# Attention softmax pacing, the start of the last value products and the cut of the last output half tile in a one-core hybrid layer step

## The chip, the cores and the metric

The kernel runs on one core of a Trainium2 chip. The core has TensorE (PE in the profile; its weight loads are PEld), VectorE (DVE), ScalarE (ACT), GpSimd (POOL) and SyncE (SP), each with its own queue of instructions, which it works through in order. SBUF is the on-chip memory of 128 partitions; PSUM holds what PE writes, in eight banks of 128 x 512 floats. The metric is the device time of one execution in microseconds; 613.63 us is the median of three runs before the change (612.94 to 613.96).

## The reference

One layer of a diffusion trunk: 1024 latent tokens and 128 own context tokens of width 1024, and 256 cached context tokens. A shared normalised and modulated input goes through one projection into a gated MLP group (A) and a latent attention group with four heads (B); both are gated, concatenated, sent through one output projection, added to the residual under a gate, and normalised. The change concerns the attention of the latent tokens and the very end of the output projection:

```python
def one_block(i):
    qn = lax.dynamic_slice_in_dim(q_nope, s0, Q_BLOCK, axis=1)
    logits = []
    for qr, (kn, kr, _) in zip(q_ropes, key_sets):      # latent keys, cached context keys
        logits.append(jnp.einsum('bqhn,bkhn->bhqk', qn, kn) + jnp.einsum('bqhr,bkr->bhqk', qrb, kr))
    s = jnp.concatenate(logits, axis=-1).astype(jnp.float32) * ATTN_SCALE
    p = jax.nn.softmax(s, axis=-1).astype(v_all.dtype)
    return jnp.einsum('bhqk,bkhv->bqhv', p, v_all)
...
y = jnp.concatenate([a_out, attn * jax.nn.silu(g_b)], axis=-1) @ w_o
return x + gate * y
...
y_prompt = _rmsnorm(xp, final_g)
```

## The kernel before

**Precision.** Every large product is made of three: each operand is split into a high part in the shorter format fp32r (`pool_copy` on POOL or a copy on ACT) and a low part, the rest (`lo_of` on DVE, line 112), and high x high, high x low and low x high are added up in PSUM.

**Written time.** The order of instructions on PE, ACT, DVE and POOL is written out by the program. A counter `now` stands for the time that PE has used so far: each step of PE adds its cost. `later(dt, fn)` puts work of the other engines on a list, due at the step's start plus dt; `catch_up` writes out what is due before the next step. So a number such as 0.6 or 2.3 does not delay anything on the chip: it decides only between which other instructions of its engine something stands. `need(key)` writes out the list, in order of due time, until the named result has been written. `merged(a, b)` interleaves two lists of steps by their shares of the cost. SP's queue of DMAs is in written order as well.

**Attention.** There are 8 tiles of 128 queries and 4 heads, 32 heads `(t, h)` in all, and 16 pairs of two heads `(t, pr)`. A round `c` of the main loop (line 1964 on) scores heads 2c+2 and 2c+3 and does the value products of pair c-1. Scoring a head is `lat(0)`, `lat(1)` (512 latent keys each, five products) and `con` (256 context keys, lines 1520 to 1524). Then `start` takes the maximum over the latent logits and `shift` that over the context logits and the bias `nb` (DVE); `exp(0)` and `exp(1)` (ACT, line 1498) write the context and the latent part of `e`, a tile of 128 x 1280, with their sums; `divide` adds the sums, takes the reciprocal (DVE) and scales `e` (POOL, line 1506). Value products of a pair go in five steps `tr(i)` and `av(i)`: `tr` transposes four blocks of `e` on PE into a PSUM bank (`pT`, line 1567; the pool `pst` has two banks, shared with the `at` products), ACT copies the high part `ph` out (line 1571), DVE makes the low part `pl`, which empties the bank; `av` (lines 1591 to 1593) lags two steps behind `tr`. `fin1` copies the sum to `os`, `fin2` multiplies it by the value projection (`at`, line 1610), and DVE multiplies the result into `mixB` (line 1612).

**Units.** From round 2 on, 16 small units (`t_unit`) prepare differences of blocks of the output weights for the last stage (a Strassen scheme); each `divide` takes one off the list `units` until it is empty. While the list is not empty, or for tile 1, the exponentials are written "apart". Later the lists `his` and `los` hold high and low parts of other splits (pieces of `w_o`, first blocks of the mixed activations); `spare_hi(n)` and `spare_lo(n)` write out up to n of them, `divide` among their callers. `need_lo` and `wo_need` write out what a product is about to read.

**The change of stage.** After the last scored head the loop ends, `need` asks for the `e` of the last two heads, the score banks are closed and five banks `psw` opened for the output projection. `tail` is then set, which lets every `low()` of a transposed block call `spare_hi` and `spare_lo`. The first output products (`early`) are interleaved with the value products of pairs 14 and 15 (tile 7). Pieces 5 to 7 of `w_o` are loaded into buffers that the attention gives free, and split in halves of 512 columns.

**The end.** The last stage is planned by a small list scheduler, `Plan`: each step has an engine, a cost, what it depends on and a priority, and the plan's run sets the order on each engine. The last products are those of the prompt tile's left half (`finish_left`): tile 8, columns 0 to 511, in two parts cut at `cut_at` (steps `pz0`, `pz1`, 24 products each). Each part is multiplied by the gate (`zm`, line 2298), added to x (`za`, line 2299), squared and summed on ACT (`sq8.0` and `zq`, lines 2103 and 2304), and multiplied by the final gain (`zf`, line 2307); `zv` (line 2308) to `zr3` make the root, `zo0` and `zo1` scale both halves and store them.

Of the kernel before, what the change touches and what calls it, by code (L numbers as in the profile page):

```python
# [20 lines left out]
NS = 8  # L21
# [73 lines left out]
def tile_hymba_step(ctx: ExitStack, tc: tile.TileContext, I, O):  # L95
# [1375 lines left out]
    def softmax(t, h, lat_, con_):  # L1471
# [11 lines left out]
        def shift():  # L1483
            V.tensor_reduce(m[:, 1:2], con_, axis=AX.X, op=ALU.max)
            if units or t < 2 or (t, h) == (NS - 1, 3):
                V.tensor_reduce(nb, m, axis=AX.X, op=ALU.max)
                V.tensor_scalar(nb, nb, nscl[:, t : t + 1], None, op0=ALU.mult)  # L1487
            else:
                V.scalar_tensor_tensor(nb, m[:, 0:1], m[:, 1:2], nscl[:, t : t + 1], op0=ALU.max, op1=ALU.mult)
            apart = bool(units) or t == 1  # L1490
            later(1.2 if apart else 0.6, lambda: exp(0))
            later(2.3 if apart else 0.6, lambda: exp(1))
            later(3.9 if apart else 3.1 if t == 0 else 2.5, divide)
            later(1.3, lambda: spare_lo(1))
# [5 lines left out]
        def divide():  # L1500
            V.tensor_tensor(rs, su[:, 0:1], su[:, 1:2], op=ALU.add)
            V.reciprocal(rs, rs)
            first = 512 if (t, h) == (NS - 1, 3) else 0
            if first:
                V.tensor_scalar(e[:, :first], e[:, :first], rs, None, op0=ALU.mult)
            G.tensor_scalar(e[:, first:], e[:, first:], rs, 0.0, op0=ALU.mult, op1=ALU.add)  # L1506
            made.add(("e", t, h))
# [18 lines left out]
    def score_steps(t, h):  # L1526
# [16 lines left out]
        def con():  # L1543
            logits(c_, (a, b, unrot), slice(CTX0, CTX0 + 256))
            later(0.95 if units or t == 1 else 0.7, cell["shift"])

# [4 lines left out]
    def value_steps(t, pr):  # L1551
# [9 lines left out]
        def tr(i):  # L1561
# [11 lines left out]
            def low():  # L1573
                lo_of(pl[:, :w], ps[:, :w], ph[:, :w])
                made.add(("p", t, pr, i))
                if tail:
                    spare_hi(1)
                    spare_lo(1)
# [75 lines left out]
    def next_load():  # L1654
# [16 lines left out]
        def ready():  # L1671
            for i in range(2):
                c_ = slice(i * 512, i * 512 + 512)
                split_job(lambda c_=c_: pool_copy(hi[:, c_], r[:, c_]), lambda c_=c_: low(c_), ("w", k, i))
# [118 lines left out]
    with tc.manual_schedule(engines=engines):  # L1793
# [170 lines left out]
        for c in range(len(pairs)):  # L1964
# [20 lines left out]
            if 2 * c + LEAD + 1 == 23:  # L1985
                for k in range(3):
                    wo_piece(2 + k, *flat[1][2 * k : 2 * k + 2])
        need(*[("e", *h) for h in heads[-2:]])
        closed(c_ps)
# [24 lines left out]
        later(2.0, lambda: [t_pieces(2, 2 * n, whole[2][:, 2048 * n + 2048 : 2048 * n + 4096]) for n in range(2)])  # L2014
        vs = value_stream(pairs[-2])
        merged(vs[:3], [])
        merged(vs[3:], early[:10])
# [258 lines left out]
    def finish_left():  # L2276
# [6 lines left out]

        cut_at = 384
        own_of = (slice(0, cut_at), slice(cut_at, 512))
# [8 lines left out]
        for j in range(2):  # L2294
            o = lambda j=j: cell[j][:, at_[j]]
            dur = (0.57, 0.3)[j]
            on_t(f"pz{j}", (4.3, 1.6)[j], lambda j=j: left(j), [], takes=("w",) if j else ("w", "w"))
            on_v(f"zm{j}", lambda o=o, c=own_of[j]: V.tensor_tensor(o(), o(), g()[:, c], op=ALU.mult), [f"pz{j}", "own0"], 0.5, dur)
# [7 lines left out]
        for j, dep in ((0, ["za1"]), (1, ["zv"])):  # L2306
            on_v(f"zf{j}", lambda j=j: V.tensor_tensor(x()[:, own_of[j]], cell[j][:, at_[j]], fg[:, own_of[j]], op=ALU.mult), [*dep, "sq8.0", "zq", "fg"] if j else [*dep, "sq8.0", "fg"], 0.6, (0.57, 0.3)[j])
        on_v("zv", lambda: V.scalar_tensor_tensor(v, ssq[(8,)][:, 2:3], 1.0 / 1024.0, v0, op0=ALU.mult, op1=ALU.add), ["zq", "zv1"], 0.4, 0.2)
# [125 lines left out]
```

## Time and profile before

| what | value |
|---|---|
| median of 3 runs | 613.63 us |
| lowest, highest | 612.94, 613.96 us |
| the profiled execution, as a run | 614.5 us |
| its span in the trace | 612.7 us |
| its mean granted PE clock | 0.992 of full speed |
| ACT, DVE, POOL busy | 330.2, 426.1, 208.4 us |
| attention stage, from the first `pT` of a pair to the last value product | about 334 to 528 us |
| last products `left`, first and last start | 598.63, 605.34 us |

The profile is of one execution, and its times count from the start of its span. A row of the timeline gives the start, the duration, the engine, the line of the kernel, the operation, output and inputs with their shapes, how many instructions are merged, and in brackets the time that the engine stood idle before it, with what ended the wait. Products on PE overlap, so the distance between two starts, not the duration, is what one costs. A row of the view by stretches gives the stretch, its length, the busy time and the number of instructions of PE, PEld, DVE, ACT and POOL, then the granted clock, the DMA share and GB/s.

### The profile page before, as it was taken

What the parts mean: (1) busy time and instruction counts of PE and PEld (TensorE: products, weight loads), DVE (VectorE), ACT (ScalarE), POOL (GpSimd) and SP (SyncE); (2) the same over time, 40 slices, a digit from 0 to 9 for tenths busy, and PEclk for the clock granted to TensorE, in tenths of its full rate; (3) what the DMA queues carried; (4) which work ended last, traced back from release to release, by engine and by line L of the source; (5) the groups of instructions that cost most, each with busy time, mean ns of one, the idle gap of its engine ahead of it and who ended that gap; (6) DMA issues with size and microseconds to landing.
All of it is one profiled execution on the core that took longest, in us unless ns stands there. A gap on an engine that the chain in (4) does not pass through costs nothing.

```text
span 612.7 us, 10225 instructions
## 1 busy us (share of the span) xinstructions
PE 599.2 (98%) x3671; PEld 542.2 (88%) x3671; DVE 426.1 (70%) x937; ACT 330.2 (54%) x765; POOL 208.4 (34%) x249
## 2 busy tenths in 40 slices
PE   7999999999999999999999999999999999999995
PEld 6777889999988999999998999999989988888885
DVE  4685467997756468466778677777678875577885
ACT  5555773335433244465577656665745553357543
POOL 2452103000000000243363354545434446359833
PEclk9899999999999999999999999999999999999999
DMA  8992010100351114100002033434231118951443
GB/s 311 390 393 81 0 35 2 35 0 1 138 207 70 70 62 167 41 1 1 1 8 70 1 112 114 150 125 139 70 120 70 35 70 293 330 201 42 147 152 141
DMA packets 31059, 67.33 MB, mean 110 GB/s; under 512 B 3344, under 2 KB 17440, under 8 KB 29984
## 3 DMA queue, kind: packets, MB, share of 16 engines
q1 hardware_dynamic: 27792, 55.93, 25.8%
q0 software_dynamic: 2352, 8.39, 4.1%
q10 hardware_dynamic: 864, 2.36, 1.2%
q8 instruction: 29, 0.48, 0.3%
q14 instruction: 22, 0.18, 0.1%
HBM read 53.45 MB, written 13.21 MB: 109 GB/s over the span
## 4 chain that ended last, share of the span: by engine, by line
PE 92%; DMA 2%; DVE 2%; ACT 1%; issue 1%; SPq 0%; ACTq 0%; DVEq 0%
PE p L954 9%; PE tp L752 8%; PE pT L1567 6%; PE tp L976 6%; PE s L1520 3%; PE o L1591 3%; PE s L1523 3%; PE s L1521 3%; PE s L1522 3%; PE s L1524 3%; PE o L1593 3%; PE o L1592 3%; PE zacc L1390 2%; PE zacc L1389 2%; PE zacc L1391 2%; PE S L1928 2%
## 5 line engine op out<-in xcount | busy, mean ns | idle before, releaser
L112 DVE TENSOR_TENSOR pl<-pT,ph 128x512 fp32r<-128x512 f32 x81 | 55.5, 687 | 38.0 <-ACT ph L1571 37.8
L1506 POOL TENSOR_SCALAR e<-e,rs 128x1280 f32<-128x1280 f32 (+1 forms) x32 | 46.9, 1466 | 101.4 <-ACT ph L1571 41.5
L1498 ACT ACTIVATE e<-s,nb,scl 128x256 f32<-128x256 f32 x64 | 56.5, 885 | 34.5 <-DVE nb L1487 18.9
L1571 ACT CAST ph<-pT 128x512 fp32r<-128x512 f32 x80 | 46.4, 589 | 42.7 <-PE pT L1567 42.0
L1237 POOL TENSOR_TENSOR kr<-z,rope 128x64 f32<-128x64 f32 x8 | 2.6, 324 | 172.1 <-ACT z L1246 172.1
L752 PE MATMUL tp<-area,w 128*128 128x384 f32 x288 | 52.4, 338 | 0.0
L752 PEld LDWEIGHTS tp<-area,w 128*128 128x128 f32 x288 | 50.3, 188 | 0.4
L1567 PE MATMUL pT<-ident,e 128*128 128x128 f32 x320 | 48.2, 273 | 1.9 <-DVE pl L112 1.9
L1591 PE MATMUL o<-ph,vh 128*128 128x256 f32 x160 | 48.2, 301 | 0.0
L1593 PE MATMUL o<-ph,vl 128*128 128x256 f32 x160 | 45.1, 282 | 0.0
L1592 PE MATMUL o<-pl,vh 128*128 128x256 f32 x160 | 45.0, 281 | 0.0
L1567 PEld LDWEIGHTS pT<-ident,e 128*128 128x128 f32 x320 | 37.5, 141 | 5.2 <-DVE pl L112 1.3
L1481 DVE TENSOR_REDUCE m<-s 128x1 f32<-128x1024 f32 x32 | 38.9, 1216 | 2.6 <-PE s L1524 2.6
L1520 PE MATMUL s<-kch,area 128*128 128x512 f32 (+2 forms) x100 | 39.2, 392 | 0.0
L1521 PE MATMUL s<-kcl,area 128*128 128x512 f32 (+2 forms) x100 | 35.3, 353 | 0.0
L1523 PE MATMUL s<-krh,area 128*128 128x512 f32 (+2 forms) x100 | 35.3, 353 | 0.0
L1522 PE MATMUL s<-kch,area 128*128 128x512 f32 (+2 forms) x100 | 35.2, 352 | 0.0
L1524 PE MATMUL s<-krl,area 128*128 128x512 f32 (+2 forms) x100 | 35.1, 351 | 0.0
L976 PE MATMUL tp<-area,w 128*128 128x384 f32 x192 | 35.0, 337 | 0.0
L976 PEld LDWEIGHTS tp<-area,w 128*128 128x128 f32 x192 | 33.6, 187 | 0.4 <-issue 0.4
L1591 PEld LDWEIGHTS o<-ph,vh 128*128 128x128 f32 x160 | 30.1, 188 | 1.6
L1592 PEld LDWEIGHTS o<-pl,vh 128*128 128x128 f32 x160 | 30.2, 189 | 1.4
(696 smaller groups left out, 1726.6 us busy)
## 6 DMA issues: line engine op xcount, KB each, us to landing
ada<-in_ada_ss SPq DMA_DIRECT2D x16, 512.0 KB, 8.0
w2r<-in_w_t SPq DMA_DIRECT2D x12, 512.0 KB, 4.3
x<-in_x SPq DMA_DIRECT2D x9, 512.0 KB, 7.4
adag<-in_ada_g SPq DMA_DIRECT2D x4, 1024.0 KB, 4.9
traw<-in_w_o SPq DMA_DIRECT2D x16, 256.0 KB, 3.1
tdram<-thi SPq DMA_DIRECT2D x32, 128.0 KB, 1.8
tdram<-traw SPq DMA_DIRECT2D x32, 128.0 KB, 1.8
wor<-in_w_o SPq DMA_DIRECT2D x8, 512.0 KB, 3.7
```

Of the source, the lines that this page charges most:

```text
L112: V.tensor_tensor(lo, src, f32(hi), op=ALU.subtract)
L752: T.matmul(tps[i, g][:, :GW], w_[i][:, k, :], x_[k, g], start=k == 0 and j == 0, stop=k == NK - 1 and j == 2)
L954: T.matmul(banks[key], a_, b_, start=k == 0 and m == 0, stop=k == 3 and m == len(passes) - 1)
L976: T.matmul(tps[c, 2][:, :GW], w_[c][:, k, :], x_[k, 2], start=k == 0 and m == 0, stop=k == NK - 1 and m == 2)
L1498: S.activation(e[:, sl], src, AF.Exp, bias=nb, scale=scl[:, t : t + 1], accum_out=su[:, i : i + 1])
L1520: T.matmul(ps, qh_, kch[:, sl], start=True, stop=False)
L1521: T.matmul(ps, qh_, kcl[:, sl], start=False, stop=False)
L1523: T.matmul(ps, qr_, krh[:, sl], start=False, stop=False)
L1567: T.transpose(ps[:, w : w + P], es[t, h][:, c * P : (c + 1) * P], ident)
L1591: T.matmul(o, vh[:, kt, :], ph[:, sl], start=c == 0, stop=False)
L1592: T.matmul(o, vh[:, kt, :], pl[:, sl], start=False, stop=False)
L1593: T.matmul(o, vl[:, kt, :], ph[:, sl], start=False, stop=c == n - 1)
```

## The change

There are three groups of edits, and the arithmetic that is done stays the same.

1. In `softmax` and `con` the spaced times now hold for every tile but the first, whether or not units are left: `shift` 0.95 (0.7 before) after the step of `con`, then `exp(0)` 1.2 (0.6), `exp(1)` 2.3 (0.6), `divide` 3.9 (2.5). For the very last head `exp(0)` is due after 0.5.
2. The first three steps of pair 14 (tile 7, first two heads) are written before `need` asks for the last division, and so before the `psw` banks are opened and `tail` is set. The last division is POOL's alone (DVE had done 512 of its 1280 columns). In the tail `low()` writes out two high parts instead of one, and pieces 5 to 7 of `w_o` are split right half first.
3. The left half of the last tile is cut at 256 instead of 384 columns, and the plan's costs for its steps are set to match.

```diff
--- before.py
+++ after.py
@@ -1487,8 +1487,9 @@
                 V.tensor_scalar(nb, nb, nscl[:, t : t + 1], None, op0=ALU.mult)
             else:
                 V.scalar_tensor_tensor(nb, m[:, 0:1], m[:, 1:2], nscl[:, t : t + 1], op0=ALU.max, op1=ALU.mult)
-            apart = bool(units) or t == 1
-            later(1.2 if apart else 0.6, lambda: exp(0))
+            apart = t > 0
+            last = (t, h) == (NS - 1, 3)
+            later(0.5 if last else 1.2 if apart else 0.6, lambda: exp(0))
             later(2.3 if apart else 0.6, lambda: exp(1))
             later(3.9 if apart else 3.1 if t == 0 else 2.5, divide)
             later(1.3, lambda: spare_lo(1))
@@ -1500,10 +1501,7 @@
         def divide():
             V.tensor_tensor(rs, su[:, 0:1], su[:, 1:2], op=ALU.add)
             V.reciprocal(rs, rs)
-            first = 512 if (t, h) == (NS - 1, 3) else 0
-            if first:
-                V.tensor_scalar(e[:, :first], e[:, :first], rs, None, op0=ALU.mult)
-            G.tensor_scalar(e[:, first:], e[:, first:], rs, 0.0, op0=ALU.mult, op1=ALU.add)
+            G.tensor_scalar(e, e, rs, 0.0, op0=ALU.mult, op1=ALU.add)
             made.add(("e", t, h))
             spare_hi(1 if his and his[0] in heavy else 2)
             spare_lo(2)
@@ -1542,7 +1540,7 @@
 
         def con():
             logits(c_, (a, b, unrot), slice(CTX0, CTX0 + 256))
-            later(0.95 if units or t == 1 else 0.7, cell["shift"])
+            later(0.95 if t else 0.7, cell["shift"])
 
         return [(1.08, lambda: lat(0)), (1.08, lambda: lat(1)), (0.55, con)]
 
@@ -1574,7 +1572,7 @@
                 lo_of(pl[:, :w], ps[:, :w], ph[:, :w])
                 made.add(("p", t, pr, i))
                 if tail:
-                    spare_hi(1)
+                    spare_hi(2)
                     spare_lo(1)
 
             later(1.15, low)
@@ -1669,7 +1667,7 @@
                 next_load()
 
         def ready():
-            for i in range(2):
+            for i in range(2) if k < 5 else (1, 0):
                 c_ = slice(i * 512, i * 512 + 512)
                 split_job(lambda c_=c_: pool_copy(hi[:, c_], r[:, c_]), lambda c_=c_: low(c_), ("w", k, i))
 
@@ -1985,6 +1983,8 @@
             if 2 * c + LEAD + 1 == 23:
                 for k in range(3):
                     wo_piece(2 + k, *flat[1][2 * k : 2 * k + 2])
+        vs = value_stream(pairs[-2])
+        merged(vs[:3], [])
         need(*[("e", *h) for h in heads[-2:]])
         closed(c_ps)
         c_pw, psw = opened("psw", bufs=5, space=PSUM)
@@ -2012,8 +2012,6 @@
         early += [(0.65, lambda k=k: product(2, first_banks[2], ks=[k])) for k in range(3)]
         later(0.5, lambda: early_split(2))
         later(2.0, lambda: [t_pieces(2, 2 * n, whole[2][:, 2048 * n + 2048 : 2048 * n + 4096]) for n in range(2)])
-        vs = value_stream(pairs[-2])
-        merged(vs[:3], [])
         merged(vs[3:], early[:10])
         merged(value_stream(pairs[-1], drain=True), early[10:])
         catch_up(1e9)
@@ -2281,7 +2279,7 @@
         g, x = (lambda: own[0][:, 0:512]), (lambda: own[0][:, 512:1024])
         on_g("z4", lambda: G.tensor_tensor(keep, keep, fg[:, R], op=ALU.mult), ["sq8.1", "fg"], 2.5)
 
-        cut_at = 384
+        cut_at = 256
         own_of = (slice(0, cut_at), slice(cut_at, 512))
         at_ = (slice(0, cut_at), slice(0, 512 - cut_at))
 
@@ -2293,8 +2291,8 @@
 
         for j in range(2):
             o = lambda j=j: cell[j][:, at_[j]]
-            dur = (0.57, 0.3)[j]
-            on_t(f"pz{j}", (4.3, 1.6)[j], lambda j=j: left(j), [], takes=("w",) if j else ("w", "w"))
+            dur = 0.43
+            on_t(f"pz{j}", 2.9, lambda j=j: left(j), [], takes=("w",) if j else ("w", "w"))
             on_v(f"zm{j}", lambda o=o, c=own_of[j]: V.tensor_tensor(o(), o(), g()[:, c], op=ALU.mult), [f"pz{j}", "own0"], 0.5, dur)
             on_v(f"za{j}", lambda o=o, c=own_of[j]: V.tensor_tensor(o(), o(), x()[:, c], op=ALU.add), [f"zm{j}"], 0.5, dur)
         square(8, 0, lambda: cell["junk"][:, own_of[0]], L, ["za0"], 0.5, lambda: cell[0][:, own_of[0]])
@@ -2304,7 +2302,7 @@
             "zq", lambda: S.activation(cell["junk"][:, own_of[1]], cell[1][:, at_[1]], AF.Square, accum_out=ssq[(8,)][:, 2:3]), ["za1"], 0.4, 0.5
         )
         for j, dep in ((0, ["za1"]), (1, ["zv"])):
-            on_v(f"zf{j}", lambda j=j: V.tensor_tensor(x()[:, own_of[j]], cell[j][:, at_[j]], fg[:, own_of[j]], op=ALU.mult), [*dep, "sq8.0", "zq", "fg"] if j else [*dep, "sq8.0", "fg"], 0.6, (0.57, 0.3)[j])
+            on_v(f"zf{j}", lambda j=j: V.tensor_tensor(x()[:, own_of[j]], cell[j][:, at_[j]], fg[:, own_of[j]], op=ALU.mult), [*dep, "sq8.0", "zq", "fg"] if j else [*dep, "sq8.0", "fg"], 0.6, 0.43)
         on_v("zv", lambda: V.scalar_tensor_tensor(v, ssq[(8,)][:, 2:3], 1.0 / 1024.0, v0, op0=ALU.mult, op1=ALU.add), ["zq", "zv1"], 0.4, 0.2)
         on_s("zr", lambda: S.activation(root, v, AF.Sqrt), ["zv"], 0.3, 0.25)
         on_v("zw", lambda: V.tensor_scalar(vn, v, -0.5, None, op0=ALU.mult), ["zv"], 0.3, 0.16)
```

## What I predict, and why

> **What bounds the kernel now.** I read the totals of the page first, then the view of waits for PE, then busy time by stretch through the attention stage, then the timeline at the places that these point to.
>
> ```profile
> span 612.7 us, 10225 instructions
> PE   599.2 (98%) x3671; PEld 542.2 (88%) x3671; DVE 426.1 (70%) x937; ACT 330.2 (54%) x765; POOL 208.4 (34%) x249
> ```
>
> ```profile
> PE pT L1567 <- DVE pl L112: 1.9, 2, 1.1
> ```
>
> PE is the bound, and the change takes no product away. It can win only where PE stands still (between the first and the last product the largest wait is this one: 1.9 us in 2 places, both ahead of transposes `pT`), where products use PE badly, or after the last product. The attention stage runs as rounds of two scored heads and one pair of value products. Cut at the same transpose of each round, they read:
>
> ```profile
> 427.95:440.04 12.09, 12.09 (x86) 11.15 (x85) 8.91 (x19) 7.63 (x16) 5.83 (x7) 1.00 0.23 77
> 440.04:453.33 13.29, 12.21 (x87) 11.13 (x85) 8.85 (x18) 7.71 (x17) 4.15 (x4) 1.00 0.48 160
> 453.52:465.52 12.00, 12.00 (x88) 11.08 (x86) 9.73 (x19) 6.67 (x16) 5.28 (x6) 1.00 0.22 87
> 465.52:477.56 12.04, 12.04 (x88) 11.12 (x86) 9.76 (x20) 6.57 (x15) 5.54 (x6) 1.00 0.14 45
> 477.56:489.69 12.13, 12.13 (x88) 11.12 (x85) 9.71 (x21) 6.61 (x15) 5.53 (x6) 1.00 0.01 1
> 489.69:501.86 12.17, 12.17 (x93) 11.37 (x91) 9.42 (x21) 6.44 (x15) 5.64 (x5) 1.00 0.14 45
> ```
>
> The columns after the length are the busy times of PE, weight load, DVE, ACT and POOL. The first of these rounds still has its exponentials spaced (units are left); from the second on, `units` is empty and they come together. Those five rounds, 11 heads (21 to 31), are what the first edit touches.
>
> **Edit 1, exponentials spaced.** The long round is 13.29, against 12.09 for a spaced round. Its timeline:
>
> ```profile
> 442.40 0.39 PE L1524 MATMUL s<-krl,area 128*128 128x512 f32 x1
> ...
> 446.24 0.60 PE L1610 MATMUL at<-os,wuv 128*128 128x128 f32 x4
> 447.93 0.63 PE L1567 MATMUL pT<-ident,e 128*128 128x128 f32 x4 [1.08 <-DVE pl L112]
> ...
> 441.88 1.08 ACT L1571 CAST ph<-pT 128x512 fp32r<-128x512 f32 x2
> ...
> 444.03 0.59 ACT L1571 CAST ph<-pT 128x512 fp32r<-128x512 f32 x1
> ...
> 442.50 0.69 DVE L112 TENSOR_TENSOR pl<-pT,ph 128x512 fp32r<-128x512 f32 x1 [2.90 <-ACT ph L1571]
> 443.11 0.15 DVE L1501 TENSOR_TENSOR rs<-su 128x1 f32<-128x1 f32 x1
> ...
> 444.78 1.21 DVE L1481 TENSOR_REDUCE m<-s 128x1 f32<-128x1024 f32 x1
> 445.91 0.68 DVE L112 TENSOR_TENSOR traw<-traw,thi 128x512 fp32r<-128x512 f32 x1
> 446.51 0.41 DVE L1484 TENSOR_REDUCE m<-s 128x1 f32<-128x256 f32 x1
> ...
> 447.10 0.68 DVE L112 TENSOR_TENSOR pl<-pT,ph 128x512 fp32r<-128x512 f32 x1
> ```
>
> The transposes wait for a PSUM bank that `pl` of the third transposes empties. Its `ph` was done at 444.62 (444.03 + 0.59), but on DVE the two maxima and a low part stand ahead of it. In written time a round's third transposes come at 4.34 and the context logits at 4.78: `pl` is due at 5.49 (+1.15), the context maximum at 5.48 (+0.70). With +0.95 it is due at 5.73, so `pl` goes first: 447.10 - 446.51 = 0.59 at least. Then, the exponentials no longer stand together ahead of two `ph` on ACT, so the `pl` at 442.50 starts soon after its own transposes, and the wide maximum can start right after its logits, which end at 442.79 (442.40 + 0.39), instead of at 444.78. From there DVE needs 1.13 (444.78 to 445.91), two one-column operations for the division (0.15 in the row, about 0.4 with the gaps), a low part (0.60, from 445.91 to 446.51) and `pl` 0.68: done near 445.6, ahead of the 446.7 or so at which PE wants the bank (446.24 plus most of the 0.60 of the four products before). I take the whole difference to a spaced round, 13.29 - 12.09 = **-1.2**; bounds -0.59 and -1.29 (to the best round, 12.00).
>
> In the other four rounds, spacing costs or gives what the rows say: they are 12.00, 12.04, 12.13 and 12.17, in sum 48.34; four spaced rounds are 48.36. **0.0**, bounds -0.3 (all down to 12.00) and +0.4 (0.1 each). The division moves from 2.65 to 4.30 of written time in the next round for the second head and from 7.98 to 9.63 for the first; its result is first read by transposes at least half a round later, 6 us, so its lateness is covered. What comes later on DVE instead is the third `pl` itself: the division, and low parts that it gives out, now stand ahead of it (the slower rival below).
>
> **Edit 2, pair 7's first transposes ahead of the last division.**
>
> ```profile
> 503.81 0.40 PE L1959 MATMUL w<-area,ml 128*128 128x512 f32 x1
> 505.07 0.66 PE L1567 MATMUL pT<-ident,e 128*128 128x128 f32 x4 [0.86 <-DVE pl L112]
> ...
> 502.22 1.20 ACT L1498 ACTIVATE e<-s,nb,scl 128x1024 f32<-128x1024 f32 x1
> ...
> 503.40 1.07 ACT L1571 CAST ph<-pT 128x512 fp32r<-128x512 f32 x2
> ...
> 504.33 1.28 DVE L112 TENSOR_TENSOR pl<-pT,ph 128x512 fp32r<-128x512 f32 x2
> ...
> 498.06 1.62 POOL L1506 TENSOR_SCALAR e<-e,rs 128x1280 f32<-128x1280 f32 x1 [2.53 <-ACT ph L1571]
> 504.10 1.09 POOL L1506 TENSOR_SCALAR e<-e,rs 128x768 f32<-128x768 f32 x1 [3.17 <-ACT ph L1571]
> ```
>
> PE's order stays: the same three steps follow the last logits either way. What changes is what ACT and DVE have queued: now `need` writes out head 31's exponentials, sums, reciprocal and DVE's part of the division before the two `ph` and `pl`. So `ph` waits until 503.40 although both banks had been filled before, and the third transposes start at 505.07 instead of 503.81 + 0.23 = 504.04: 1.03 lost. Afterwards the first `ph` stands ahead of the small exponential (due 0.50 against 0.90), the second ahead of the wide one (1.59 against 2.70), and both `pl` ahead of the division (1.15 and 2.24 against 4.30). **-1.03**; bounds -1.03 and -0.4 (if one `pl` still stands behind 0.6 of other DVE work).
>
> The price: the wide exponential of head 31 ends one `ph` later (about 0.55), and POOL divides all 1280 columns: 1.62 for 1.09, so POOL's later work, two DMA issues of the T pieces included, shifts by up to 1.1. Nothing reads that `e` before pair 15's transposes, behind all of pair 14's. Where the delay could reach PE is the split of the sixth weight piece:
>
> ```profile
> 512.38 0.64 POOL L115 TENSOR_SCALAR kch<-wor 128x512 fp32r<-128x512 f32 x1
> ...
> 514.28 0.68 DVE L112 TENSOR_TENSOR kcl<-wor,kch 128x512 fp32r<-128x512 f32 x1
> ...
> 515.24 0.40 PE L1958 MATMUL w<-kcl,area 128*128 128x512 f32 x1
> ```
>
> Here `kcl` ends at 514.96 and PE reads it at 515.24. PE comes about 1 us earlier now, POOL up to 1.1 later. The edit gives the needed right half out first (the former second of two, so one copy of 0.64 and one low part of 0.68 sooner) and two high parts per low part in the tail. That covers roughly 1.3 of about 1.8 to 2.1 at its worst. I take **+0.2**, bounds 0 and +0.9.
>
> **Edit 3, the last half tile as 256 and 256.**
>
> ```profile
> 598.63 0.33 PE L1957 MATMUL left<-area 128*128 128x384 f32 x1
> ...
> 602.82 0.22 PE L1957 MATMUL left<-area 128*128 128x128 f32 x1
> ...
> 605.34 0.28 PE L1959 MATMUL left<-area,ml 128*128 128x128 f32 x1
> ...
> 444.37 0.28 PE L1591 MATMUL o<-ph,vh 128*128 128x256 f32 x1
> ...
> 444.96 0.28 PE L1593 MATMUL o<-ph,vl 128*128 128x256 f32 x1
> ...
> 605.65 0.30 DVE L2298 TENSOR_TENSOR left<-left,own 128x128 f32<-128x128 f32 x1 [1.34 <-PE left L1959]
> 607.12 0.16 DVE L2308 SCALAR_TENSOR_TENSOR smalls<-fss,smalls 128x1 f32<-128x1 f32 x1
> 447.70 0.41 DVE L1612 TENSOR_TENSOR mixB<-mixB,at 128x256 f32<-128x256 f32 x1
> ...
> 604.28 0.47 ACT L2103 ACTIVATE junk<-left 128x384 f32<-128x384 f32 x1 [1.15 <-DVE left L2299]
> 606.32 0.26 ACT L2304 ACTIVATE junk<-left 128x128 f32<-128x128 f32 x1
> ```
>
> The 24 products of 384 columns take 602.82 - 598.63 = 4.19, 0.175 each; the 24 of 128 take 2.52 for 23 steps, 0.110 each, 2.63 in all. A third of the columns costs 63% of the time: small products stand near a floor. Products of 256 columns with a fresh weight load each run in the value products: 444.37 to 444.96 is 0.59 for 5 steps, 0.118 each. 48 of them: 5.66 for 6.82, **-1.16**. Bounds: -1.16, and 0 if they lie on the straight line between the two sizes (0.142 x 48 = 6.8).
>
> A rule of the Trainium skill (TensorE: Matmul & The Clock Gate, Back-to-back issue gap) speaks against this edit: the page gives a sustained spacing of 81 ns at 128 columns and 131 ns at 512, and on a line between them 256 columns cost an estimated 97 and 384 an estimated 114, so that both cuts need about 4.7 us and nothing is won. The trace has 0.110 and 0.175 for its 128 and 384, so I do not go by it.
>
> Behind the last product the widths go up: the product with the gate and the sum with x each 0.41 for 0.30 (by the row of this width), the square about 0.37 (between 0.26 and 0.47) for 0.26, one scaling 0.41 for 0.30: +0.44. Against that, 605.65 to 607.12 is 1.47 for a chain whose links are shorter: tile 7's last root step and tile 8's first sum stand in it, because tile 8's first part was ready only just before. With the first part ready some 1.3 earlier they can be done before: about -0.3. Chain together +0.1, bounds -0.1 and +0.45. I take **-1.06** for the edit.
>
> **Sum:** -1.2 + 0.0 - 1.03 + 0.2 - 1.06 = -3.1. The profiled execution has 612.7 of span in a run of 614.5, which is 0.87 above the median 613.63; its span would be 609.6, and the median 613.63 - 3.1 = **610.5**. The best ends of all bounds give -1.29 - 0.3 - 1.03 - 1.26 = -3.9 (609.7).
>
> **Rivals.**
> *Slower: DVE's new order stalls the third `pl`.* Place: each spaced round, where the division and up to two low parts now stand ahead of that `pl`. Computed above with one low part it has 1.1 us to spare, with two 0.5. It decides when a low part there must wait for its high part, which POOL makes only behind a division of 1.62 and up to two copies of 0.64, 2.9 in all. Then `pl` is some 1.9 later, PE stands about 1.4 in each of the four rounds that split weights: +5.6 and the -1.2 not won fully; -3.1 + 5.6 = +2.5, **616.1**. For it: DVE is busy 9.4 to 9.8 of 12 there. Against it: a low part is written out 1.6 after its high one and then waits for the next free place, and the earlier spaced rounds with their `traw` low parts run at 12.09. Chance 0.10.
>
> *256 columns lie on the line.* No gain on PE, so 610.5 + 1.16 = **611.7**. Against it: the 0.118 of products of just this width. It is also what the line through the Trainium skill's two spacings would give (TensorE: Matmul & The Clock Gate, Back-to-back issue gap). Chance 0.09.
>
> *The wait of edit 2 moves to the sixth weight piece.* Its gain is given back there up to 0.9 instead of 0.2: **611.2**; with a further part of edit 1's lost, 611.7. Chance 0.17.
>
> *The change does not do what it says:* the order on DVE stays such that both waits come back in another bank, and only edit 3 counts or two such losses meet: 613.63 - 1.06 = **612.6**, no change that can be told. Chance 0.08.
>
> **How the numbers follow.** My forecast (all three gain; 609.6 to 611.0) has 0.56. Faster here is below 612.4, since about 0.2% can be told from no change: 0.56 + 0.09 + 0.17 = 0.82; same 0.08; slower 0.10. The range goes from 609.4 (the best ends and a little spread of the runs, 612.94 to 613.96) to 612.2, which takes in the two faster rivals.
>
> **What would show it.** Edit 1: the round now at 440 to 453 reads 12.0 to 12.2, and no wait of PE for `pl` is left there; wrong if the rounds after it grow beyond 12.3. Edit 2: `ph` of pair 14's first transposes lies ahead of the last small exponential, PE's third transposes follow without idle time, POOL has 32 divisions of 1280 columns; wrong if PE waits at `kcl`. Edit 3: 48 products at 0.118, 5.7 from the first to the last; wrong if they take 6.8, or if from the last product to the end it takes over 0.5 more than now. The forecast as a whole fails if PE's waits in the attention stage again sum to 1.9 or more.

## The result, and the profile after

The changed kernel takes 609.55 us (median of 6 runs, 608.48 to 611.09), the kernel before in the same comparison 613.29 (6 runs, 612.18 to 614.14): ratio 0.9942, 95% interval 0.9923 to 0.9962, or 3.74 us less. I had predicted 610.5 with a range of 609.4 to 612.2.

The profiled execution of the changed kernel took 608.9. Its page begins:

```profile
span 607.1 us, 10219 instructions
PE 595.5 (98%) x3671; PEld 538.9 (89%) x3671; DVE 428.4 (71%) x936; ACT 331.6 (55%) x765; POOL 208.6 (34%) x249
...
L1504 POOL TENSOR_SCALAR e<-e,rs 128x1280 f32<-128x1280 f32 x32 | 47.1, 1472 | 98.9 <-ACT ph L1569 48.0
```

The count of products is the same 3671, and POOL now makes all 32 divisions over 1280 columns. The view of waits for PE is down to what lies ahead of the attention stage (`warm` 1.4 us, `xT` 1.3, `modp` 0.7 and 0.5, `vacc` 0.4). The line `pT <- DVE pl` of 1.9 us in 2 places is gone, and nothing has taken its place there. The stage shows the same. The view by stretches, cut from the first transposes `pT` of a kernel's own pairs to the first product `S` of the last stage, reads for the kernel before (line numbers differ a little from kernel to kernel)

```profile
326.92:529.94 203.02, 201.07 (x1376) 183.38 (x1375) 147.51 (x312) 117.02 (x242) 92.86 (x99) 1.00 0.34 112
```

and for the changed kernel

```profile
325.17:525.31 200.14, 200.08 (x1377) 183.24 (x1375) 150.46 (x311) 118.36 (x242) 93.08 (x99) 1.00 0.35 115
...
432.33:444.40 12.07, 12.07 (x85) 11.13 (x84) 8.96 (x19) 7.75 (x16) 5.83 (x6) 1.00 0.27 89
444.40:456.39 11.99, 11.99 (x86) 11.08 (x84) 9.27 (x18) 6.92 (x14) 4.13 (x5) 1.00 0.35 104
456.39:468.38 11.99, 11.99 (x86) 11.08 (x85) 10.63 (x20) 6.92 (x14) 5.54 (x7) 1.00 0.24 90
468.38:480.36 11.98, 11.98 (x85) 11.07 (x84) 10.62 (x20) 6.92 (x14) 5.53 (x7) 1.00 0.11 40
480.36:492.35 11.99, 11.99 (x86) 11.07 (x84) 10.63 (x21) 6.93 (x14) 5.55 (x8) 1.00 0.00 0
```

PE stood idle for 203.02 - 201.07 = 1.95 in the stage and now stands 0.06. Its busy time falls by 0.99 as well (201.07 to 200.08), with as many products (1376 and 1377): the end of a product that reaches into a wait counts as busy (ahead of the long round's transposes the step was 1.25 longer, with 1.08 idle), so the idle time alone is less than what the stage gains. The lower five rows are rounds, from the start of one `at` to the start of the next; the first of them still has units left, the second is the former long one. Cut the same way, the kernel before has 13.28, 11.99, 12.05 and 12.13 in rows two to five. (The prediction's rows were cut at a transpose; its long round read 13.29.)

This pair of profiles differs by 612.7 - 607.1 = 5.6 of span, more than the runs do. Of that, 326.92 - 325.17 = 1.75 lies ahead of the stage, in code that the change leaves alone; over all profiles of this study that start lies anywhere from 324.09 to 327.41. The traces show where most of it arises. In the profile before, PE waits 1.09 for its first `ada` from DMA (at 10.04), and the granted clock is 0.54 from 12 to 16 us and 0.61 from 16 to 20; in the profile after, PE doesn't wait there (9.88) and the clock is 1.00 in both stretches. Products `vacc` start 0.43 apart in the one (17.36, 17.79) and 0.23 in the other (14.60, 14.83), and by about 25 us the two kernels are 1.42 apart. Over the 14 profiles, the five with 1.00 in both stretches start the stage at 324.09 to 325.35, the nine with less at 325.09 to 327.41. Ahead of that first product the nine waited 0.57 to 1.55 and the five 0 to 0.60; that the wait is what lowers the clock is not shown. So I compare kernels by the stretches behind it, each from the start of one product to the start of another:

| us | before | after | difference |
|---|---|---|---|
| first `pT` to first `S` | 203.02 | 200.14 | -2.88 |
| first `S` to first `left` | 68.69 | 68.70 | 0.0 |
| first `left` to last `left` | 6.71 | 5.63 | -1.08 |
| last `left` to the end | 7.36 | 7.46 | +0.10 |
| sum | | | -3.86 |

The sum agrees with the 3.74 of the runs. The timeline of the changed kernel in the former long round:

```profile
444.40 0.60 PE L1608 MATMUL at<-os,wuv 128*128 128x128 f32 x4
444.84 0.60 PE L1565 MATMUL pT<-ident,e 128*128 128x128 f32 x4
...
441.09 1.22 DVE L1481 TENSOR_REDUCE m<-s 128x1 f32<-128x1024 f32 x1
...
442.48 0.69 DVE L112 TENSOR_TENSOR traw<-traw,thi 128x512 fp32r<-128x512 f32 x1
443.09 0.69 DVE L112 TENSOR_TENSOR pl<-pT,ph 128x512 fp32r<-128x512 f32 x1
443.69 0.42 DVE L1484 TENSOR_REDUCE m<-s 128x1 f32<-128x256 f32 x1
444.14 0.25 DVE L1489 SCALAR_TENSOR_TENSOR nb<-m,nscl 128x1 f32<-128x1 f32 x1
```

The order on DVE is the one that I had laid out: wide maximum, the two one-column operations of the division (not among these rows), one low part, third `pl`, and only then the context maximum. `pl` ends at 443.78 and PE wants the bank at 444.84: 1.06 to spare, and the transposes follow the products `at` by 0.44 instead of 1.69. Pair 14:

```profile
500.29 0.39 PE L1957 MATMUL w<-area,ml 128*128 128x512 f32 x1
500.52 0.60 PE L1565 MATMUL pT<-ident,e 128*128 128x128 f32 x4
497.53 0.59 ACT L1569 CAST ph<-pT 128x512 fp32r<-128x512 f32 x1 [1.15 <-PE pT L1565]
498.01 0.57 ACT L1499 ACTIVATE e<-s,nb,scl 128x256 f32<-128x256 f32 x1
498.67 0.59 ACT L1569 CAST ph<-pT 128x512 fp32r<-128x512 f32 x1
499.15 1.22 ACT L1499 ACTIVATE e<-s,nb,scl 128x1024 f32<-128x1024 f32 x1
```

Each `ph` stands ahead of an exponential, and the third transposes come 0.23 after the product before them, where it was 1.26. The sixth weight piece, whose high and low part are `kch` and `kcl`:

```profile
510.31 0.48 PE L1955 MATMUL w<-kch,area 128*128 128x512 f32 x1
510.85 0.50 PE L1956 MATMUL w<-kcl,area 128*128 128x512 f32 x1
509.68 2.13 DVE L112 TENSOR_TENSOR kcl<-wor,kch 128x512 fp32r<-128x512 f32 x2
```

The step from `kch` to `kcl` is 0.54, where it was 0.32 before: 0.22 is given back. And the end:

```profile
594.01 0.28 PE L1955 MATMUL left<-area 128*128 128x256 f32 x1
596.88 0.28 PE L1955 MATMUL left<-area 128*128 128x256 f32 x1
599.64 0.28 PE L1957 MATMUL left<-area,ml 128*128 128x256 f32 x1
599.96 0.43 DVE L2296 TENSOR_TENSOR left<-left,own 128x256 f32<-128x256 f32 x1 [1.25 <-PE left L1957]
601.40 0.16 DVE L2306 SCALAR_TENSOR_TENSOR smalls<-fss,smalls 128x1 f32<-128x1 f32 x1 [0.15 <-ACT junk L2302]
```

The first 24 products of 256 columns take 2.87, 0.120 each.

### The profile page after: what moved, and what is told of

Read it like the earlier page. It is cut to its first block, busy times and chain, and to the rows that moved or that the text cites. A ratio compares the mean times of both kernels' runs of the same rounds, so it can differ in the third digit from the quotient of the medians.

```text
span 607.1 us, 10219 instructions
## 1 busy us (share of the span) xinstructions
PE 595.5 (98%) x3671; PEld 538.9 (89%) x3671; DVE 428.4 (71%) x936; ACT 331.6 (55%) x765; POOL 208.6 (34%) x249
## 4 chain that ended last, share of the span: by engine, by line
PE 92%; DVE 2%; DMA 1%; POOL 1%; ACT 1%; issue 1%; SPq 0%; POOLq 0%; DVEq 0%; ACTq 0%
PE p L954 10%; PE tp L752 8%; PE tp L976 6%; PE pT L1565 5%; PE s L1518 3%; PE s L1519 3%; PE s L1521 3%; PE s L1520 3%; PE s L1522 3%; PE o L1589 3%; PE o L1590 3%; PE o L1591 3%; PE zacc L1390 2%; PE zacc L1389 2%; PE zacc L1391 2%; PE S L1926 2%
## 5 line engine op out<-in xcount | busy, mean ns | idle before, releaser
L1504 POOL TENSOR_SCALAR e<-e,rs 128x1280 f32<-128x1280 f32 x32 | 47.1, 1472 | 98.9 <-ACT ph L1569 48.0
```

## The experiments

Stage below means the first row of the table above. A time of one run is given beside it where it was taken alone. The ratios are the comparison's own, over all its runs, and not quotients of the two medians.

**Each group of edits alone.** First the spacing, with the earlier small exponential for the last head:

```diff
-            apart = bool(units) or t == 1
-            later(1.2 if apart else 0.6, lambda: exp(0))
+            apart = t > 0
+            last = (t, h) == (NS - 1, 3)
+            later(0.5 if last else 1.2 if apart else 0.6, lambda: exp(0))
...
-            later(0.95 if units or t == 1 else 0.7, cell["shift"])
+            later(0.95 if t else 0.7, cell["shift"])
```

> The kernel before with edit 1 alone (spaced times for every tile but the first, the context maximum due 0.95, the last head's context exponential due 0.5). Theory (DVE reaches the third pl of a round in time once maxima and exponentials are spaced): the long round of 13.28 reads 12.0 to 12.1, the other four stay between 11.9 and 12.1, the stretch from the first transposes to the last scored head shrinks by 1.2 to 1.5; the wait of 1.03 ahead of pair 14's third transposes stays; time about -1.3 (ratio 0.998). Rival (the wait only moves, because the division now stands ahead of the third pl): some round after it reads over 12.3, or the wait at pair 14 grows beyond 1.3, and the time changes by less than 0.5.

Measured: 611.03 against 613.62 before, ratio 0.9969 (0.9956 to 0.9983); stage 200.97, -2.05. Its rounds are 11.98, 11.99, 11.98 and 11.99. The gain is larger than the 1.3 that I had expected. The wait at pair 14 stays, only smaller:

```profile
500.50 0.40 PE L1960 MATMUL w<-area,ml 128*128 128x512 f32 x1
...
501.62 0.66 PE L1568 MATMUL pT<-ident,e 128*128 128x128 f32 x4 [0.72 <-DVE pl L112]
```

It is 1.12 from start to start, against 1.26 before.

Then the transposes ahead of the division, with everything that belongs to that group:

```diff
-            first = 512 if (t, h) == (NS - 1, 3) else 0
...
+            G.tensor_scalar(e, e, rs, 0.0, op0=ALU.mult, op1=ALU.add)
...
-                    spare_hi(1)
+                    spare_hi(2)
...
-            for i in range(2):
+            for i in range(2) if k < 5 else (1, 0):
...
+        vs = value_stream(pairs[-2])
+        merged(vs[:3], [])
         need(*[("e", *h) for h in heads[-2:]])
```

> The kernel before with edit 2 alone (pair 14's first three steps written ahead of need, the last division on POOL alone, two high parts per low part, right half of pieces 5 to 7 first). Theory: the long round stays at 13.28, the wait ahead of pair 14's third transposes goes (1.03), a small wait of 0.1 to 0.4 at the sixth weight piece comes; time about -0.9 (ratio 0.9985). Rival (without spaced exponentials the exponentials of head 31, due 0.6, still stand ahead of both ph): the wait stays at 0.8 or more.

Measured: 613.36, ratio 0.9993 (0.998 to 1.0006), which can't be told from no change; stage 202.41, -0.61. The wait at pair 14 is gone, and the sixth piece takes 0.74 of its 1.03 back, where I had expected 0.1 to 0.4 (the rest of the stage's gain lies in steps of about 0.1):

```profile
513.24 0.48 PE L1954 MATMUL w<-kch,area 128*128 128x512 f32 x1
514.30 0.50 PE L1955 MATMUL w<-kcl,area 128*128 128x512 f32 x1 [0.58 <-DVE kcl L112]
```

1.06 from start to start: 0.74 given back when alone, 0.22 together with the spacing. The timelines of the two kernels show a reason. Here POOL starts the first copy `kch` at 512.47, which is 9.02 behind pair 14's third transposes (503.45), and DVE stands idle for 0.86 until that copy ends; in the changed kernel it starts at 508.45, 7.93 behind them (500.52). POOL's sum `mixB<-mixA`, 1.28 long, stands behind the last division here (505.90) and ahead of it in the changed kernel (497.69). This is read from two timelines; no run tests it alone.

Then the cut of the last half tile:

```diff
-        cut_at = 384
+        cut_at = 256
...
-            dur = (0.57, 0.3)[j]
+            dur = 0.43
```

> The kernel before with edit 3 alone (cut at 256 and 256). Theory: 48 products start 0.118 apart, 5.55 from the first start to the last against 6.71; from the last start to the end of the span about 7.45 against 7.36; time -1.0 to -1.1 (ratio 0.9983). Rival (straight line between 128 and 384 columns): 0.142 apart, 6.7 from the first to the last, time +0.1.

Measured: 611.83, ratio 0.9978 (0.9966 to 0.9989); stage 202.97 (before 203.02), `left` 5.63, to the end 7.50. The stages of the first two alone sum to -2.66 against -2.88 for all together; the product of the three ratios is 0.9940 against the measured 0.9942. The parts nearly add up, and the spacing helps the others by some 0.2.

**The two halves of the spacing.** The kernel before with only the time of `shift`:

```diff
-            later(0.95 if units or t == 1 else 0.7, cell["shift"])
+            later(0.95 if t else 0.7, cell["shift"])
```

> The kernel before with one number of edit 1: the context maximum due 0.95 instead of 0.70 for all tiles but the first; exponentials and divisions stay together. Theory (the maximum ahead of pl costs 0.6, the late ph the rest): the long round reads 12.6 to 12.8. Rival A (the maximum is the whole cause): 12.1. Rival B (the exponentials ahead of ph are the whole cause): 13.2 to 13.3.

Measured: stage 204.89, 1.87 longer than before (615.57 in one run, the kernel before 612.3 beside it). The long round is 13.06, from 13.28, and the one behind it 12.61, from 11.99. The timeline in the latter:

```profile
467.99 0.66 PE L1567 MATMUL pT<-ident,e 128*128 128x128 f32 x4 [0.43 <-DVE pl L112]
...
465.45 1.20 ACT L1498 ACTIVATE e<-s,nb,scl 128x1024 f32<-128x1024 f32 x1
466.63 1.07 ACT L1571 CAST ph<-pT 128x512 fp32r<-128x512 f32 x2
...
467.25 0.69 DVE L112 TENSOR_TENSOR pl<-pT,ph 128x512 fp32r<-128x512 f32 x1 [1.78 <-ACT ph L1571]
```

The gap that I wanted closed shrinks from 1.69 to 1.05, against 0.44 without a wait. The exponentials, still together, are now due 0.25 later, and the wide one stands on ACT ahead of two `ph` (465.45 and 466.63), for whose low part the transposes at 467.99 wait. The next two rounds wait at the same place, so that the three behind the long one take 12.61 to 12.74 instead of 11.99 to 12.13; the fourth, 12.52 for 11.98, waits at the first output product and at pair 14. With 13.06 the long round lies between what I had expected (12.6 to 12.8) and the rival of the exponentials (13.2 to 13.3): the maximum and the exponentials each have a part in it.

The other half, the changed kernel with the old time of `shift`:

```diff
-            later(0.95 if t else 0.7, cell["shift"])
+            later(0.95 if units or t == 1 else 0.7, cell["shift"])
```

> The changed kernel with the context maximum due 0.70 again when no units are left (spaced exponentials and divisions stay). Theory (with ph early, DVE has 1.1 us to spare at the third pl, and the maximum ahead of it takes 0.6 of them): all rounds stay at 11.9 to 12.2. Rival A (the place of the maximum decides): the rounds after the units read 12.4 or more.

Measured: stage 205.37, 5.23 longer than the changed kernel (613.05 in one run). The view of waits has one line for it, and the timeline shows one of the five places:

```profile
PE pT L1565 <- DVE pl L112: 4.3, 5, 1.0
```

```profile
457.55 0.63 PE L1565 MATMUL pT<-ident,e 128*128 128x128 f32 x4 [0.66 <-DVE pl L112]
...
454.92 0.67 DVE L112 TENSOR_TENSOR area<-wor,area 128x512 fp32r<-128x512 f32 x1
455.51 0.42 DVE L1484 TENSOR_REDUCE m<-s 128x1 f32<-128x256 f32 x1
455.96 0.84 DVE L1489 SCALAR_TENSOR_TENSOR nb<-m,nscl 128x1 f32<-128x1 f32 x1
456.73 0.68 DVE L112 TENSOR_TENSOR pl<-pT,ph 128x512 fp32r<-128x512 f32 x1
...
455.20 1.60 POOL L1504 TENSOR_SCALAR e<-e,rs 128x1280 f32<-128x1280 f32 x1 [4.06 <-DVE rs L1503]
```

My expectation, rounds of at most 12.2, fell, and the rival that the place of the maximum decides held. The spaced division brings a low part ahead of the context maximum, and both stand ahead of `pl`. So the two halves need each other: the later `shift` without spacing loses 1.87 against the kernel before, spacing without it 205.37 - 203.02 = 2.35 (although it has the second group's edits too), both together win 2.05. I had not expected the size: `nb`, one column, takes 0.84 here and ends (456.80) just when POOL's division does. Of the ten `nb` of this form five take 0.83 or 0.84, one 0.53 and four 0.23 to 0.25; in the changed kernel all ten take 0.23 to 0.26.

To test that reading, the same kernel with `nb` as two instructions with one tensor operand each (the scale goes in as the scalar of each partition; the diff is against the changed kernel):

```diff
-            if units or t < 2 or (t, h) == (NS - 1, 3):
+            if True:
                 V.tensor_reduce(nb, m, axis=AX.X, op=ALU.max)
                 V.tensor_scalar(nb, nb, nscl[:, t : t + 1], None, op0=ALU.mult)
             else:
                 V.scalar_tensor_tensor(nb, m[:, 0:1], m[:, 1:2], nscl[:, t : t + 1], op0=ALU.max, op1=ALU.mult)
...
+            later(0.95 if units or t == 1 else 0.7, cell["shift"])
```

> As e5_spaced_due70, but the bias nb made in two operations that each read one SBUF tensor, for all heads, instead of one that reads two. New theory (in e5 that one-column operation took 0.84 where it takes 0.22 elsewhere, because it ran into POOL's division of e and had to wait for its end): the waits for pl ahead of the fourth transposes shrink by about 0.5, rounds of 12.3 to 12.6 instead of 12.84 to 13.11. Rival (only the place of the context maximum counts): rounds stay at 12.8 to 13.1 or grow by the extra operation (0.15).

```profile
457.98 0.16 DVE L1486 TENSOR_REDUCE nb<-m 128x1 f32<-128x2 f32 x1
458.17 0.21 DVE L1487 TENSOR_SCALAR nb<-nb,nscl 128x1 f32<-128x1 f32 x1
...
457.22 1.60 POOL L1504 TENSOR_SCALAR e<-e,rs 128x1280 f32<-128x1280 f32 x1 [4.07 <-DVE rs L1503]
```

Two instructions under the same division take 0.16 and 0.21, less than the one. Rounds 12.75, 12.39, 12.79 and 12.81 instead of 13.05, 12.84, 13.03 and 13.11, stage 203.94, -1.43: the stretched `nb` is there, but it is only 0.24 to 0.45 of each round's loss of 0.85 to 1.12. The rest, by the rows, is the order itself: the low part and the maximum still stand ahead of `pl`. I had expected rounds of 12.3 to 12.6, and one of the four is that short.

**The parts of the second group.** The kernel before with only the move:

```diff
+        vs = value_stream(pairs[-2])
+        merged(vs[:3], [])
         need(*[("e", *h) for h in heads[-2:]])
...
-        vs = value_stream(pairs[-2])
-        merged(vs[:3], [])
```

> The kernel before with the move of pair 14's first three steps alone: the last division still shared by DVE and POOL, one high part per low part, left halves first. Theory (it is the order of ph and pl against head 31's division that costs): the wait ahead of the third transposes is gone or under 0.2, as in the whole edit, though at the sixth weight piece PE may wait 0.3 to 1.2. Rival (DVE's share of the division is what delays pl): the wait stays at 0.5 or more, since DVE still does 512 columns (0.49).

Measured: stage 204.08, 1.06 longer than before (614.63 in one run). Its waits in the output products:

```profile
PE w L1958 <- DVE krl L112: 0.9, 1, 0.9
PE w L1958 <- DVE kcl L112: 0.7, 1, 0.7
```

Pair 14's wait is gone, and the sixth and seventh pieces are late by more than it was. The other parts of the group are what makes the move pay. Taken back one at a time in the changed kernel, first the order of the halves and then the second high part:

```diff
-            for i in range(2) if k < 5 else (1, 0):
+            for i in range(2):
```

> The changed kernel with pieces 5 to 7 split left half first again. Theory: the right half, which PE reads first, comes one copy (0.6) and one low part (0.7 to 1.4) later, the distance at the sixth weight piece grows from 0.54 to between 1.2 and 1.9. Rival (both halves are written ahead of PE's product anyway and it waits for the later one): it stays at 0.5 to 0.6.

```diff
-                    spare_hi(2)
+                    spare_hi(1)
```

> The changed kernel with one high part per low part in the tail. Theory (two keep POOL ahead of PE): the right half of the sixth piece comes later on POOL, the distance there grows from 0.54 to 0.8 or more, and a wait at the seventh piece appears. Rival (what PE reads is written out by wo_need in time either way): stage lengths within 0.1 of the changed kernel.

```profile
514.31 0.50 PE L1956 MATMUL w<-kcl,area 128*128 128x512 f32 x1 [1.06 <-DVE kcl L112]
```

```profile
520.60 0.50 PE L1927 MATMUL f<-area,ringB 128*128 128x512 f32 x1 [0.59 <-DVE area L112]
```

Left half first (the upper row): stage 201.57, +1.43 (612.57 in one run), and the step at the sixth piece is 1.54 instead of 0.54. One high part (the lower row): stage 200.99, +0.85 (610.85 in one run); but the step at the sixth piece gets shorter, 0.34 instead of 0.54, and the loss stands later, at the left half of a later piece, where PE's step between two products `f` of the last pair is 0.98. A loss was expected and came, but not at the place where I had put it.

The division, shared with DVE again (in the changed kernel):

```diff
+            first = 512 if (t, h) == (NS - 1, 3) else 0
+            if first:
+                V.tensor_scalar(e[:, :first], e[:, :first], rs, None, op0=ALU.mult)
-            G.tensor_scalar(e, e, rs, 0.0, op0=ALU.mult, op1=ALU.add)
+            G.tensor_scalar(e[:, first:], e[:, first:], rs, 0.0, op0=ALU.mult, op1=ALU.add)
```

> The changed kernel with the last division shared again (DVE 512 columns, POOL 768). Theory (POOL's lateness is what PE meets at the sixth weight piece): POOL is 0.25 earlier, the distance between the two products there falls from 0.54 to 0.32 to 0.40, first transposes to last stage 0.1 to 0.2 shorter. Rival (the low part there is slowed by DVE and POOL working at the same time): it stays at 0.5.

```profile
510.24 0.48 PE L1958 MATMUL w<-kch,area 128*128 128x512 f32 x1
510.56 0.48 PE L1959 MATMUL w<-kcl,area 128*128 128x512 f32 x1
```

The step is 0.32 again, the stage 199.94, -0.20, the span 606.9. So without POOL's longer division (1.35 for 1.10) the 0.22 at the sixth piece is gone. It is gone too with one high part (0.34) and where PE comes there 0.9 later (0.31, in the next kernel): what counts, by these three, is POOL's split against PE's arrival, and the division is one part of it. This is the best version by its stage; the one run (608.63) can't tell 0.2 from nothing.

The small exponential of the last head, as late as the others:

```diff
-            later(0.5 if last else 1.2 if apart else 0.6, lambda: exp(0))
+            later(1.2 if apart else 0.6, lambda: exp(0))
```

> The changed kernel without the special 0.5 for the last head's context exponential (due 1.2 as for the others). Theory (the first output product takes the PSUM bank that this exponential reads): it now stands behind the second ph, and PE waits 0.4 to 0.9 ahead of the first output product. Rival (that product takes another bank): no wait there, stage lengths as in the changed kernel.

```profile
499.94 0.50 PE L1955 MATMUL w<-area 128*128 128x512 f32 x1 [0.57 <-ACT e L1499]
```

Stage 200.75, +0.61 (609.62 in one run): the first output product waits for that exponential, 0.86 for 0.12 from start to start.

**What products of other widths cost.** The changed kernel cut at 320 and 192:

```diff
-        cut_at = 256
+        cut_at = 320
```

> The changed kernel with the last half tile cut at 320 and 192 columns. Theory (a floor of about 0.11 per product, and above some 250 columns 0.45 ns per column): 0.146 and 0.112 apart, 6.1 from the first start to the last against 5.63, the chain behind 0.1 to 0.2 shorter, time about +0.35. Rival (256 is a width that runs well by itself, others lie on the line between 128 and 384): 0.159 and 0.126, 6.75 in all, time +1.0.

```profile
595.15 0.30 PE L1955 MATMUL left<-area 128*128 128x320 f32 x1
598.67 0.25 PE L1955 MATMUL left<-area 128*128 128x192 f32 x1
601.22 0.28 PE L1957 MATMUL left<-area,ml 128*128 128x192 f32 x1
```

24 products of 320 columns take 3.52, 0.147 each; 23 steps of 192 take 2.55, 0.111 each. First to last `left` is 6.07, and from there to the end 7.18: 13.25 for the two, 13.09 in the changed kernel (610.23 in one run). That is 0.16 longer where I had expected 0.35; the costs of the products came as expected, and the rest behind them is shorter than expected.

## Why the prediction was right

Its steps, one by one:

- **Long round, -1.2:** measured -1.29 (13.28 to 11.99), at its better bound. The order on DVE and the 1.1 to spare were as worked out (1.06). But the sentence that the later place of the maximum alone gives "0.59 at least" fell. At the place itself it gives 0.64 (1.69 to 1.05), the round as a whole gains only 0.22 and the stage loses 1.87, because the exponentials behind the maximum move with it. That was a bound on one wait, used as a bound on the round. The 0.59 is also no more than a part of the wait: with the late exponentials the place still holds PE up by 0.61 (1.05 against 0.44).
- **The other four rounds, 0.0:** mis-sized. The three that follow the long one gain 0.21 (36.17 to 35.96). The fourth runs into the output products and can't be cut alike; up to `S` the spacing alone takes 0.49 from that last stretch (34.25 to 33.76), of which 0.15 at the transposes behind `at`, where small waits had been, 0.14 at pair 14 and the rest in steps of about 0.1. I had put a spaced round at 12.09, but that row still held the work of units: rounds with units stay at 12.07, spaced rounds without them run at 11.98 to 11.99. The row was the right form of round with another load; that the units cost the 0.08 is argued from these rounds, and no run takes the units out.
- **Pair 14, -1.03:** the step fell from 1.26 to 0.23, so -1.03. ("Pair 7" in the heading of that step is a slip; it is the first pair of tile 7.) **Sixth piece, +0.2:** +0.22 in the changed kernel. The causes were right in the main: the shared division takes it away, the order of the halves holds off another 1.0 there. But the second high part, which I had counted as cover at this piece, makes the step there longer (0.54, 0.34 without it) and pays at a later piece. And POOL's last division takes 1.35 here, not the 1.62 of the forecast. What I took for cover is more than that: without the second high part and the right half first, the move alone costs 1.06. And the cover depends on the spacing, 0.74 without it.
- **Cut, -1.06:** `left` -1.08, behind it +0.10, so -0.98. The products cost 0.120 and not 0.118. The chain from the first product with the gate to the one-column operation is 1.44 (599.96 to 601.40) for 1.47, wider links and one link fewer in front, as argued; the wider last scaling makes up the rest.

Where the forecast was 3.1 the runs show 3.74. Most of the difference is the second step, about 0.5 in the rounds and transposes that I had set at nothing.

The slower rival fell: no round of the four is above 12.0, and DVE's 10.6 of 12 busy there is no bound. It is near, though: the order with the early `shift` makes rounds of 13 from the same amount of work. The line rival fell (256 columns 0.120, not 0.142). A line between the two spacings that the Trainium skill gives (TensorE: Matmul & The Clock Gate, Back-to-back issue gap) would have given no gain either, as an estimate; the trace does not agree with it for these products (0.110 at 128 columns, where the page has 81 ns). The rival of the sixth piece is right for the second group alone, where 0.74 comes back and the runs show no gain; together with the spacing it is 0.22. That the change doesn't do what it says fell with the waits.

What stays open: why the clock ahead of the stage differs from profile to profile, and whether POOL's earlier sum is all that makes the sixth piece less late under the spacing.

## What to carry to other kernels

A due time in a hand-written order is worth nothing by itself: ask for each edit what else is queued behind the moved instruction on its engine, and try the edit's halves alone before you call one of them the cause. When a comparison row is taken for a new state, look whether it carries the same load. When work is moved forward past a division or a copy, look at the next split that this engine owes, and bring its order forward too.

## What the hardware showed that I had not expected

A one-column instruction can take as long as the rest of another engine's wide one. In the kernel with the early `shift`, `nb` (two tensor operands, `m` and `nscl`, both in SBUF) began 0.76 into POOL's division (455.20 + 1.60) and ended with it, 0.84 long, where it takes 0.22 with POOL standing still (446.96 in the kernel before); as two instructions with one tensor operand each, under a division of the same length, they took 0.16 and 0.21. It is no single case: in the kernels before, changed and with the early `shift`, every `nb` of this form that begins under a division or a copy of POOL ends within 0.02 of that instruction's end, the 0.23 to 0.26 of the changed kernel too. There the order puts `nb` at the last quarter of a microsecond of the division. The Trainium skill (SBUF — State Buffer, Who interferes with whom) says that a VectorE instruction with two SBUF inputs contends with a GpSimd instruction that reads SBUF, and that the shared ports are an exclusive lock; these rows agree.

Products with a fresh weight load each do not cost by a line in their columns: 0.110 at 128, 0.111 at 192, 0.120 at 256, 0.147 at 320 and 0.175 at 384 (granted clock 1.00 in each). Up to 192 columns there is no gain in being narrower, and from 256 to 384 each 64 columns cost 0.027 to 0.028, so that two equal cuts at the knee were the best of the three cuts tried.
